# Twelve of sixteen gate projections of a merge, computed earlier and kept in DRAM

## The chip, the core and the metric

The kernel runs on one core of one Trainium2 chip. A core has a tensor engine (PE, with its weight load PEld), a vector engine (DVE), a scalar engine (ACT), GpSimd (POOL), and SyncE (SP), which issues most DMA transfers. Each engine works through its own instructions in a fixed order; semaphores tie them together. The metric is the device time of one execution in microseconds (us), lower is better. The kernel before takes 2801.38 us (median of 3 runs, 2801.16 to 2807.91).

## What is computed

512 tokens and 16 meta tokens of 1024 features go through two blocks; only the first block's mixer matters here. In float32, with RMS norms left out of the sketch:

```
z = norm(h) @ w_in
c_q, c_kv, k_pe, r_q, r_k, r_v, r_g, za, zr = split(z)
y_a = attention(c_q, c_kv, k_pe) @ w_mla_out      # 8 heads, causal, latent queries and keys
y_r = retention(r_q, r_k, r_v, r_g) @ w_ret_out   # 8 heads, in chunks of 128 tokens
merged = sigmoid(za) * y_a + sigmoid(zr) * y_r    # za, zr: [tokens, 1024]
h = h + merged @ w_mix_out
```

Then come an expert layer (128 x 128 experts, sixteen picked per head), a second block with three kinds of attention, and a feed-forward layer.

## The kernel before

Every activation lies as [128 features, tokens], 1024 features being 8 tiles. Every large product is done in three passes with operands split into a rounded high part and a low rest (`fm`, line 249: high x high, high x low, low x high), so a product of 128 columns of weights with 512 tokens is 3 x 8 = 24 matmuls. `wfm` brings a chunk of weights: SP loads it (line 222), ACT writes the high part (line 210), DVE or POOL in turn the low part (line 211). There are two buffers each of raw, high and low parts, and two PSUM banks `mm` for such products; a bank is free again when an engine has read the product.

The mixer, in the order of the program:

- The latent queries and keys (to about 62 us of the span).
- `ret_k(0)` to `ret_k(3)`: keys of two retention heads each. Two products of 24 matmuls (264 tokens each), a copy by ACT (line 621), four transfers between partitions issued by ACT (line 630), two products with rotation tables on DVE (lines 631, 632), POOL's sum into `rkf` (line 637), and four transposes on PE (line 640).
- Between them `mla_q(c)`: queries of four attention heads, four token tiles of nine matmuls (line 258), rotated by DVE and POOL (line 405), transposed (line 564); and `mla_kv(c)`: keys and values, five token tiles, whose norm needs a square root on ACT (line 594), products on DVE and POOL (line 598), transposes (line 603).
- `mla_attend(i, c)`: four token tiles i for each half c of the heads. Scores on PE (line 682), masked maxima on DVE (line 683), exponentials on ACT (line 694), scaling on DVE (line 700), small copies on POOL (line 701), transposes (lines 704, 713), copies (706, 715), and products with the values (708, 718). `ret_q(0)` to `ret_q(3)`, the retention's queries, stand before and among them.
- The retention's values and gate, then four chunks `ret_chunk(t)` of two half tiles each: scores `s` (line 769), DVE's mask (772), products `py` (778, 779), statistics (783, 784), normed `ry` on ACT and DVE (792, 795), transposes (799), a product on DVE (801), and the state's update (807, 810).
- The merge: for each of 8 column tiles c a gate of `za`, the attention's projection (12 matmuls), a gate of `zr`, the retention's projection (24 matmuls), and `merged`. A gate is 24 matmuls of the normed tokens `hn` and a tanh on ACT (line 831), since sigmoid is (1 + tanh of the half) / 2.

The functions write the instructions in this order; a scheduler then places each engine's instructions by its own estimate of when they are ready, so pieces of later steps come in between, and the order on an engine is fixed when the kernel runs. Names such as `mm`, `tp`, `s` and `o` are PSUM banks, `t` and `m` are tiles from the pools `t2` (5 buffers) and `mtwo` (9 buffers), which many short lives share: the scores of an attention tile take four of the nine.

Of the kernel before, what the change touches and what calls it, by code (L numbers as in the profile page):

```python
# [9 lines left out]
F32 = mybir.dt.float32  # L10
# [8 lines left out]
T = 512          # tokens whose outputs are wanted  # L19
M = 16           # meta tokens; in the key order they come after the tokens  # L20
# [6 lines left out]
GT = 3           # token tile whose experts are gathered; the others go through all experts  # L27
TD = 3 * P       # tokens that go through all experts
TB = 16          # tokens of one block of gates in DRAM
NTB = TD // TB  # L30
NE = 8           # e1's of one load of gates
SLOT = 8 * L     # words of a large slot


# ---------------------------------------------------------------- layout on the host
# [16 lines left out]
def _constants():  # L52
# [5 lines left out]
    tri01 = (q[None, :] >= q[:, None]).astype(f)                       # [m, c]  # L58
# [28 lines left out]
    c, s = (x.T.astype(np.float64) for x in _rope_tab(pos, 32))        # [32, token]  # L87
    lg = np.log(1.0 - 2.0 ** (-5.0 - np.arange(8)))
    e = lg[:, None] * pos[None, :]                                     # log of the decay since the start
    ret = np.zeros((8, P, 2, L))  # L90
    for x in range(8):                                                 # keys' pairs of heads, then queries'
        for b in range(2):
            d = np.exp(e[2 * (x % 4) + b])[None]
            d = d if x >= 4 else 64 ** -0.5 / d
            ret[x, b * 64:b * 64 + 64, 0] = np.concatenate([c, c], 0) * d
            ret[x, b * 64:b * 64 + 64, 1] = np.concatenate([-s, s], 0) * d
# [9 lines left out]
def _layout(i):  # L106
    i = {k: np.asarray(v) for k, v in i.items()}
    a = _constants()
    h = np.concatenate([i["x"][0], i["meta_tokens"]], 0)               # [528, 1024]
# [36 lines left out]
    pe = np.stack([i["pe_k_2"][0], i["pe_v_2"][0]], 0)                  # [2, 32, 64]  # L146
    pe = pe.transpose(2, 0, 1).reshape(64, 64)
    a["pe"] = np.ascontiguousarray(np.concatenate([pe, pe], 0))          # [(g dh), (k/v, l)]
    a["w_c1"] = np.stack([i[n][0].reshape(2, 16, 64, 256).transpose(0, 2, 1, 3).reshape(P, 16 * 256)  # half, dh, l, hidden
# [16 lines left out]
# ---------------------------------------------------------------- the program  # L166
def build(tc, A, OUT):
# [29 lines left out]
    # constants  # L197
# [10 lines left out]
    def split(src, hi, lo, lo_eng=None):  # L208
        """hi is src rounded to float32r, lo the rest."""
        S.copy(hi, src)  # L210
        (lo_eng or V).tensor_tensor(lo, src, hi.bitcast(F32), op=OP.subtract)  # L211
# [6 lines left out]
    def weights(ap, n, lo_pool=3, tag="w"):  # L218
        """One chunk of weights from DRAM, split in two float32r parts."""
# [14 lines left out]
    def wfm(name, c, kt=KD, width=P, c0=0):  # L234
        """some columns of weights, by tiles of features"""
        n = kt * width
        return kview(weights(A[name][c][:, c0:c0 + n], n, 2), kt, width)
# [7 lines left out]
    def fm(out, w, act, c0, t0, n, kt=KD, hooks=()):  # L245
        """out [128 columns of w, n tokens]; hooks: what comes after the first, the second pass"""
# [7 lines left out]
    def tm(out, w, act, c0, n, t0, m, kt=KD):  # L254
        """out [m tokens, n columns of w]"""
# [8 lines left out]
    def rstd_cols(sqs, n, width, out, first=0, after=None):  # L264
        """out[token, tile] = 1 / sqrt(mean over the features + eps) of the tokens from first up to n; sqs(t0, m):
        the squares of m tokens, [feature, token]; after: a factor of the tokens that comes first, and into out."""
# [17 lines left out]
    def ks(t):  # L284
        """the tiles [128, tokens] of t [128, k, tokens]"""
# [4 lines left out]
    class Squares:  # L290
        """sum of the squares of the tiles [128 features, n tokens] of the residual stream, as they come"""
# [3 lines left out]
        def add(self, x, eng=None, a=0, b=None, last=False):  # L295
            """the last tile's squares stay by themselves"""
# [12 lines left out]
    class Norm:  # L309
        """RMS norm over the features (partitions and tiles) of the tiles src, some tokens after the others;  # L310
        put(k, tile, a, b): tokens a .. b of a normed tile."""
        def __init__(self, src, sqs, g0, put, pieces=HALVES, dst=None):
# [3 lines left out]
            S.activation(self.col[:, 7:8], eps, AF.Sqrt)    # (its table is in place when the norm needs it)  # L316
            self.rowt = two(sqs.tp, "row")

        def cols(self, i):
            """1 / sqrt(mean + eps) of each token"""  # L320
# [3 lines left out]
        def row(self, i):  # L324
            """the same, along the partitions"""
# [31 lines left out]
    def by_halves(act, jobs, hooks=()):  # L357
        """products of act with columns of weights, jobs: (weights, first column, done(ps, a, b)); all jobs for
        half of the tokens, then for the other; hooks: what comes within the first product"""
# [7 lines left out]
    def residual(get, act, sqs=None, norm=None):  # L367
        """adds act's product with the weights get(k) (and their first column) to the residual stream; the last
        tiles by halves of the tokens, with the first half's norm among the products of the second"""
# [20 lines left out]
    def rope_op(dst, src, c, sn, sp, shape, tp, add=None):  # L390
        """dst = rotation of src, both [m, heads, 2 * half]; c, sn, sp: cos, -sin, sin"""
# [15 lines left out]
    def rope_tab(rope, off, w, m, h):  # L407
        """views of a packed table [cos | cos | -sin | sin], the same for each head"""
# [9 lines left out]
    def two(tp, name="t2", dt=F32):  # L418
        """a tile of 2 KB a partition, of a kind shared by many short lives"""
        return tp.tile([P, L], dt, name=name, tag="t2")  # L420

    # halves of arrays [feature, token]: the residual stream, and the experts' inputs
# [6 lines left out]
    hd = dp.tile([KD, P, T], F32, name="hd")                # the residual stream, while the experts run  # L429
    weight_pool(es, D)  # L430


    # ================================================================ first block: mixer
# [24 lines left out]
    # the latents come from the tokens before their norm, which goes into the latents' own: y = h gain / rms(h), and  # L458
    # rms of a latent c of y is sqrt(r^2 mean(c'^2) + eps), r = 1 / rms(h), c' = the latent of h gain
# [20 lines left out]
    # latent queries and keys, [feature, token], gained but not yet normed  # L480
# [27 lines left out]
    # shared rotary key, [token, 32]  # L508
# [25 lines left out]
    # four heads at a time: queries [96, head, token], their norm in the scale of the scores; keys  # L534
    # [96, head, (meta, token)]; values [token, head, 64]
# [4 lines left out]
    # the values of the meta tokens, one block of rows and columns per head  # L540
# [66 lines left out]
    # ---- retention: the decay since the start of the sequence is in the rotations' tables  # L607
    xh, qz = halves("rq", "xa")                             # queries of a head, zeros for the pair's other head
# [3 lines left out]
    kf = half_slot("rkf")                                   # keys [two heads' 64, pair, token]  # L612
    ktm = half_slot("rkt")[:, :, :T]                        # keys [token, tile (the last: meta), head's 64]

    def fm_pieces(w, pieces):
        """128 columns of w, [column, token]"""
# [7 lines left out]
    def ret_rope(x, j, n):  # L624
        """rotation of two heads [2 x 64, n tokens], the terms of a sum"""
# [23 lines left out]

    ret_k(0)  # L650
    mla_q(0)
    ret_k(1)
    va = flat(half_slot("va"), NT * 512).rearrange("p (t h d) -> p t h d", t=NT, h=8)
    mla_kv(0, va)
    ret_k(2)
    mla_q(1)
    ret_k(3)
    mla_kv(1, va)
    ret_q(0)
    pms = []  # L660
    for j in range(2):                                      # meta tokens' probabilities of four heads, zero elsewhere
# [6 lines left out]
    def mla_attend(i, c):  # L668
        """a tile of queries, four heads"""
# [946 lines left out]
```

## Time and profile before

| | |
|---|---|
| median of 3 runs | 2801.38 us |
| span of the profiled execution | 2800.6 us |
| PE busy | 2628.7 us, 94% |
| DVE busy | 1794.0 us, 64% |
| ACT busy | 1131.5 us, 40% |
| POOL busy | 1196.4 us, 43% |
| mixer, latent projections and first attention | about 60 to 230 us |
| retention's chunks | about 326 to 373 us |
| merge and output projection | about 373 to 560 us |

The page lists no time of the profiled execution beside its span; the median is 0.8 us above the span. A busy PE is a PE with a matmul under way: matmuls overlap, so the time from one start to the next says more than the length of one. The granted clock is that of PE as a share of 2.4 GHz; 0.5 is its lower level, 1.2 GHz. A wait in brackets is idle time of the engine ahead of the row and the instruction that ended it.

### The profile page before, as it was taken

What the parts mean: (1) busy time and instruction counts of PE and PEld (TensorE: products, weight loads), DVE (VectorE), ACT (ScalarE), POOL (GpSimd) and SP (SyncE); (2) the same over time, 40 slices, a digit from 0 to 9 for tenths busy, and PEclk for the clock granted to TensorE, in tenths of its full rate; (3) what the DMA queues carried; (4) which work ended last, traced back from release to release, by engine and by line L of the source; (5) the groups of instructions that cost most, each with busy time, mean ns of one, the idle gap of its engine ahead of it and who ended that gap; (6) DMA issues with size and microseconds to landing.
All of it is one profiled execution on the core that took longest, in us unless ns stands there. A gap on an engine that the chain in (4) does not pass through costs nothing.

```text
span 2800.6 us, 37220 instructions
## 1 busy us (share of the span) xinstructions
PE 2628.7 (94%) x13809; PEld 2246.1 (80%) x13809; DVE 1794.0 (64%) x3334; ACT 1131.5 (40%) x2064; POOL 1196.4 (43%) x831
## 2 busy tenths in 40 slices
PE   7889999998889799999999999998999999999998
PEld 6668778898789788888888888887666687878886
DVE  5673442259899736888988988896698521533333
ACT  4462343243777533333333333333566422422322
POOL 2322132325455926666666666662333333211111
PEclk9999999999999899999999999998999999999998
DMA  3312123322345467888888888884210132222221
GB/s 112 101 54 83 65 72 127 114 85 96 121 142 170 128 228 281 305 313 321 316 310 305 314 319 300 299 285 147 81 37 20 38 98 98 105 84 104 92 93 58
DMA packets 166149, 449.67 MB, mean 161 GB/s; under 512 B 14544, under 2 KB 67152, under 8 KB 159312
## 3 DMA queue, kind: packets, MB, share of 16 engines
q1 hardware_dynamic: 125648, 308.31, 32.0%
q0 software_dynamic: 36864, 134.23, 14.1%
q10 hardware_dynamic: 3456, 4.76, 0.7%
q8 instruction: 108, 1.77, 0.2%
q14 instruction: 73, 0.60, 0.1%
HBM read 413.10 MB, written 29.36 MB: 158 GB/s over the span
## 4 chain that ended last, share of the span: by engine, by line
PE 33%; DVE 22%; issue 9%; DMA 5%; POOL 4%; ACT 3%; ACTq 0%; DVEq 0%; SPq 0%; POOLq 0%
PE mm L249 21%; DVE vl L211 4%; PE py L1144 4%; PE pu L249 3%; DVE oh L1063 3%; DVE yg L958 2%; DVE row L948 2%; DMA row<-in_u_rows_dram,eg 2%; DMA row<-in_v_rows_dram,eg 2%; POOL oh L1038 1%; DVE al L211 1%; ACT ah L210 1%; PE tp L1469 1%; DVE act L1134 1%; PE o L1474 1%
## 5 line engine op out<-in xcount | busy, mean ns | idle before, releaser
L211 POOL TENSOR_TENSOR wl<-wr,wh 128x1024 fp32r<-128x1024 f32 (+1 forms) x199 | 480.7, 2416 | 572.6 <-ACT wh L210 277.2
L210 ACT CAST wh<-wr 128x1024 fp32r<-128x1024 f32 (+2 forms) x271 | 275.1, 1015 | 326.7 <-PE mm L249 213.3
L249 PE MATMUL pu<-xf,wh 128*128 128x384 f32 x2048 | 398.2, 345 | 0.4 <-ACT wh L210 0.4
L249 PEld LDWEIGHTS pu<-xf,wh 128*128 128x128 f32 x2048 | 366.2, 192 | 7.5 <-ACT wh L210 0.6
L210 ACT CAST ah<-act 128x384 fp32r<-128x384 f32 x128 | 65.9, 515 | 484.9 <-DVE act L1134 484.9
L211 DVE TENSOR_TENSOR al<-act,ah 128x384 fp32r<-128x384 f32 x128 | 201.7, 1576 | 79.6 <-ACT ah L210 78.3
L943 POOL DMA_INDIRECT row<-in_v_rows_dram,eg x128 | 193.6, 1512 | 132.6 <-DVE yg L958 101.5
L943 POOL DMA_INDIRECT row<-in_u_rows_dram,eg x128 | 185.4, 1449 | 130.8 <-DVE row L948 108.2
L1144 PE MATMUL py<-vh,ah 128*128 128x512 f32 x768 | 201.7, 397 | 26.7 <-ACT ah L210 26.6
L249 PE MATMUL pu<-xf,wl 128*128 128x384 f32 x1024 | 207.1, 344 | 5.3 <-POOL wl L211 5.3
L211 DVE TENSOR_TENSOR vl<-vr,vh 128x1024 fp32r<-128x1024 f32 x128 | 172.7, 1349 | 52.4 <-ACT vh L210 52.4
L1144 PE MATMUL py<-vl,ah 128*128 128x512 f32 x768 | 198.8, 394 | 0.0
L1144 PE MATMUL py<-vh,al 128*128 128x512 f32 x768 | 196.5, 390 | 0.0
L1144 PEld LDWEIGHTS py<-vh,ah 128*128 128x128 f32 x768 | 142.2, 189 | 60.3 <-ACT ah L210 37.7
L249 PEld LDWEIGHTS pu<-xf,wl 128*128 128x128 f32 x1024 | 184.4, 192 | 6.3 <-POOL wl L211 6.3
L958 DVE SCALAR_TENSOR_TENSOR yg<-row,ag,yg 128x1024 f32<-128x1024 f32 x127 | 167.9, 1322 | 16.4 <-DMA row<-in_v_rows_dram,eg 14.3
L948 DVE SCALAR_TENSOR_TENSOR row<-row,xg 128x1024 f32<-128x1024 f32 x128 | 168.4, 1346 | 10.8 <-DMA row<-in_u_rows_dram,eg 10.6
L1144 PEld LDWEIGHTS py<-vl,ah 128*128 128x128 f32 x768 | 146.2, 190 | 31.2
L1144 PEld LDWEIGHTS py<-vh,al 128*128 128x128 f32 x768 | 145.2, 189 | 30.4
L210 ACT CAST vh<-vr 128x1024 fp32r<-128x1024 f32 x128 | 134.3, 1049 | 78.8 <-DMA vr<-in_v_rows_dram 42.3
L1063 DVE TENSOR_TENSOR oh<-iota,eT 128x1024 f32<-128x1024 f32 x96 | 150.5, 1589 | 18.0 <-PE mm L1072 17.6
L211 POOL TENSOR_TENSOR wwl<-wwr,wwh 128x2048 fp32r<-128x2048 f32 x10 | 45.9, 4594 | 266.4 <-ACT wwh L210 266.4
(461 smaller groups left out, 5253.8 us busy)
## 6 DMA issues: line engine op xcount, KB each, us to landing
wr<-in_u_T_dram SPq DMA_DIRECT2D x128, 512.0 KB
vr<-in_v_rows_dram SPq DMA_DIRECT2D x128, 512.0 KB
wwr<-in_w_f_dram SPq DMA_DIRECT2D x32, 1024.0 KB
gates<-stg SPq DMA_DIRECT2D x24, 1024.0 KB
gin<-gates SPq DMA_DIRECT2D x16, 1536.0 KB
wr<-in_w_gm_dram SPq DMA_DIRECT2D x16, 512.0 KB
wr<-in_w_rv_dram SPq DMA_DIRECT2D x8, 512.0 KB
wr<-in_w_rg_dram SPq DMA_DIRECT2D x8, 512.0 KB
```

The source lines that it names most:

```text
L210: S.copy(hi, src)
L211: (lo_eng or V).tensor_tensor(lo, src, hi.bitcast(F32), op=OP.subtract)
L249: TE.matmul(out, w[a][k][:, c0:c0 + P], act[b][k][:, t0:t0 + n], start=i == 0 and k == 0, stop=i == 2 and k == kt - 1)
L943: G.indirect_dma_start(out=r, out_offset=None, in_=src, in_offset=bass.IndirectOffsetOnAxis(ap=eg[:, k:k + 1], axis=0))
L948: V.scalar_tensor_tensor(r, r, 1.0, xg, op0=OP.mult, op1=OP.mult, accum_out=ag[:, k:k + 1])
L958: V.scalar_tensor_tensor(yg[0], r, ag[:, k:k + 1], yg[0], op0=OP.mult, op1=OP.add)
L1038: G.tensor_tensor(ov[:, h], ov[:, h], iv[:, 4 * c + h, None].to_broadcast([P, 16, 16]), op=OP.mult)
L1063: V.tensor_tensor(a1, iota[:, None, None, :].to_broadcast([P, 2, 4, P]), eT[:, :2, b0 + q0:b0 + q0 + 4, None].to_broadcast([P, 2, 4, P]), ...
L1134: V.tensor_tensor(av, av, gated_acts.g[:, :, (e % NE) * TB:(e % NE + 1) * TB], op=OP.mult)
L1144: TE.matmul(py[2 * t + d], x[:, t * P:(t + 1) * P], w[:, d * 512:(d + 1) * 512], start=e == 0 and i == 0, stop=e == P - 1 and i == 2)
L1469: TE.transpose(pt[:, x * P:(x + 1) * P], sts[a][br][:, j * P:(j + 1) * P], ident)
L1474: TE.matmul(po[b * 64:b * 64 + 64, :2 * P], vt[:, j, br, g], pT[:, b * 256:b * 256 + 256], start=False, stop=last, skip_group_check=True)
```

## The change

`gate` is defined before the latent projections' loop. A generator `ahead` computes twelve gates, the eight of `za` and the first four of `zr`, into tiles of the pool `mtwo` and writes each (256 KB) to the DRAM tile `gz`. `fill(n)` takes the next n of them: one or two after most of the latent projections (six in all), one after every attention tile but the first of each half (six). In the merge `gate_of` reads a stored gate back from DRAM in place of computing it; the last four gates of `zr` are computed there as before. The rest of the difference takes comments and docstrings out and moves line numbers: line 640 of before is line 641 after, 564 is 565, 603 is 604, 621 is 622, 682 is 709, 778 is 808, 799 is 829; the tanh's line 831 is now 656.

```
+    gz = dp.tile([2, KD, P, T], F32, name="gz")
...
+    def gate(name, c, x):
+        w = wfm(name, c)
+        ps = mmps()
+        fm(ps, w, hn, 0, 0, T)
+        S.activation(x, ps, AF.Tanh, scale=0.5)
+        return x
+    AWAY = [(0, c) for c in range(KD)] + [(1, c) for c in range(4)]
+    def ahead():
+        for b, c in AWAY:
+            nc.sync.dma_start(gz[b, c], gate(("w_za", "w_zr")[b], c, mtwo("gz")[:, :T]))
+            yield
+    side = ahead()
+    def fill(n):
+        for _ in range(n):
+            next(side, None)
     ret_k(0)
     mla_q(0)
+    fill(1)
     ret_k(1)
     va = flat(half_slot("va"), NT * 512).rearrange("p (t h d) -> p t h d", t=NT, h=8)
     mla_kv(0, va)
+    fill(1)
     ret_k(2)
+    fill(1)
     mla_q(1)
+    fill(1)
     ret_k(3)
     mla_kv(1, va)
+    fill(2)
     ret_q(0)
...
     for c in range(2):
         for i in range(NT):
             mla_attend(i, c)
+            if i:
+                fill(1)
         ret_q(1 + c)
     ret_q(3)
+    fill(len(AWAY))
...
-    def gate(name, c, x):
-        w = wfm(name, c)
-        ps = mmps()
-        fm(ps, w, hn, 0, 0, T)
-        S.activation(x, ps, AF.Tanh, scale=0.5)
-        return x
...
+    def gate_of(b, c):
+        x = two(t2)[:, :T]
+        if (b, c) not in AWAY:
+            return gate(("w_za", "w_zr")[b], c, x)
+        nc.sync.dma_start(x, gz[b, c])
+        return x
     for c in range(KD):
-        x = gate("w_za", c, two(t2)[:, :T])
+        x = gate_of(0, c)
         gated("w_mla", c, oT, 4, x)
-        y = gate("w_zr", c, two(t2)[:, :T])
+        y = gate_of(1, c)
         gated("w_ret", c, yr, KD, y)
         merged(x, y, mg, c)
```

The first place is PE around the third retention key. In the kernel before, `mm_1067` is the second half of that key's product, `q_...` are the second round's queries (36 matmuls, of which the last nine are shown), `mm_1105` takes the key's transposes, and `mm_1253` is the fourth key:

```order
L249 MATMUL mm_1067<-hnh_159,wl_1037 128x264 x5
...
L258 MATMUL q_1212<-wh_1114,cqh_171 128x384 x2
L258 MATMUL q_1212<-wh_1120,cqh_171 128x384
L258 MATMUL q_1212<-wh_1114,cql_172 128x384 x2
L258 MATMUL q_1212<-wh_1120,cql_172 128x384
L258 MATMUL q_1212<-wl_1115,cqh_171 128x384 x2
L258 MATMUL q_1212<-wl_1121,cqh_171 128x384
L640 MATMUL mm_1105<-cstt_60,rkf_594 128x128 x3
L640 MATMUL mm_1105<-cstt_60,rkf_594 16x128
L564 MATMUL tp_1148<-cstt_60,m2_1138 96x128 x4
```

And now, where `mm_1136` is that half of the key's product, `mm_1174` takes its transposes, and `mm_1188` is a gate:

```order
L249 MATMUL mm_1136<-hnh_160,wl_1106 128x264 x8
L258 MATMUL q_1228<-wh_1217,cqh_172 128x384 x2
L258 MATMUL q_1257<-wh_1217,cqh_172 128x384 x2
L258 MATMUL q_1286<-wh_1217,cqh_172 128x384 x2
L641 MATMUL mm_1174<-cstt_60,rkf_595 128x128 x3
L641 MATMUL mm_1174<-cstt_60,rkf_595 16x128
L249 MATMUL mm_1188<-hnh_160,wh_1184 128x512 x8
L249 MATMUL mm_1188<-hnl_161,wh_1184 128x512 x4
L249 MATMUL mm_1188<-hnl_162,wh_1184 128x512 x4
L249 MATMUL mm_1188<-hnh_160,wl_1185 128x512 x8
L258 MATMUL q_1228<-wh_1223,cqh_172 128x384
```

Between the key's product and its transposes stand six matmuls of queries in place of thirty-six; the other thirty come behind a gate.

The second place is ACT just ahead of that, in the changed kernel alone. `mm_1076` is the second gate, `mm_1110` and `mm_1136` are the two halves of the third key's product, `rk` is the square root of the keys' norm, `kT` the copies of their transposes:

```order
L606 COPY kT_928<-tp_1031 96x4x128
L622 COPY t2_1109<-mm_1110 128x264
L595 ACTIVATE rk_1054<-rk_1054,epst_63 16x4
L656 ACT_TABLE_LOAD
L656 ACTIVATE gz_1069<-mm_1076 128x512
L606 COPY kT_928<-tp_1063 96x4x16
L210 CAST wh_1217<-wr_1215 128x768
L622 COPY t2_1109<-mm_1136 128x264
```

The tanh that frees the bank of `mm_1076`, which `mm_1136` takes over, stands behind the copy of `mm_1110`, a square root and the load of a table.

The third place is PE in the retention's chunks. `py` are the chunk's products, `s` the scores, `tp` the transposes; before, `mm_3550` is the attention's first projection and `mm_3571` the first gate of `zr`:

```order
L249 MATMUL mm_3550<-oTl_1522,wh_3546 128x512 x2
L249 MATMUL mm_3550<-oTh_1521,wl_3547 128x512 x4
L249 MATMUL mm_3571<-hnh_159,wh_3567 128x512 x4
L778 MATMUL py_3470<-rv_2260,sT_3468 128x128
L779 MATMUL py_3470<-wst_3421,rq_585 128x128
...
L799 MATMUL tp_3456<-cstt_60,ry_3451 128x128
L249 MATMUL mm_3571<-hnh_159,wh_3567 128x512 x2
L799 MATMUL tp_3456<-cstt_60,ry_3451 128x128
L249 MATMUL mm_3571<-hnh_159,wh_3567 128x512
```

And now, from the last matmul of that projection (`mm_3928`) on:

```order
L249 MATMUL mm_3928<-oTh_1726,wl_3925 128x512
L829 MATMUL tp_3675<-cstt_60,ry_3670 128x128 x2
L808 MATMUL py_3742<-rv_2669,sT_3740 128x128
L809 MATMUL py_3742<-wst_3735,rq_585 128x128
...
L799 MATMUL s_3779<-rq_586,rkf_595 128x256 x2
L829 MATMUL tp_3717<-cstt_60,ry_3712 128x128 x4
L808 MATMUL py_3784<-rv_2669,sT_3782 128x128
L809 MATMUL py_3784<-wst_3735,rq_586 128x128
```

The gates that lay between the chunk's steps are gone; from the fifth of the eight half tiles on, no matmul of another step stands between them.

## Rows read from the trace of the kernel before

**Rows 1.** Windows: length, busy (count) by engine, granted clock, DMA share, GB/s.

```profile
60.00:230.00 170.00, 150.41 (x960) 119.51 (x958) 110.40 (x335) 83.77 (x192) 48.95 (x68) 0.97 0.27 82
...
156.00:228.00 72.00, 67.26 (x457) 49.61 (x456) 51.84 (x182) 40.39 (x98) 17.49 (x37) 0.98 0.18 56
...
325.60:373.50 47.90, 46.04 (x304) 37.56 (x304) 35.31 (x118) 23.03 (x41) 12.51 (x9) 1.00 0.09 28
...
373.50:556.00 182.50, 179.82 (x792) 145.59 (x791) 42.50 (x50) 53.03 (x67) 53.46 (x32) 1.00 0.34 114
```

**Rows 2.** Waits of PE from 60 to 230 us: total, times, longest.

```profile
PE mm L640 <- POOL rkf L637: 6.2, 4, 2.5
PE tp L564 <- POOL m L405: 3.5, 2, 2.1
PE s L682 <- DVE mx L683: 3.3, 1, 3.3
PE tp L603 <- POOL m L598: 2.8, 4, 1.6
PE tp L603 <- DVE rk L593: 1.1, 1, 1.1
```

**Rows 3.** Timeline of PE: ends of key products, and their transposes.

```profile
88.71 1.16 PE L249 MATMUL mm<-hnh,wl 128*128 128x264 f32 x8
...
96.91 0.66 PE L640 MATMUL mm<-cstt,rkf 128*128 128x128 f32 x4 [1.47 <-POOL rkf L637]
...
107.84 0.86 PE L249 MATMUL mm<-hnh,wl 128*128 128x264 f32 x5
...
117.65 0.66 PE L640 MATMUL mm<-cstt,rkf 128*128 128x128 f32 x4 [0.67 <-POOL rkf L637]
```

**Rows 4.** Timeline of ACT: a copy, a square root, the table load, the next operation.

```profile
127.95 0.37 ACT L621 COPY t<-mm 128x264 f32<-128x264 f32 x1
...
152.57 0.30 ACT L594 ACTIVATE rk<-rk,epst 16x4 f32<-16x4 f32 x1 [0.73 <-DVE rk L593]
...
155.90 0.21 ACT L605 COPY kT<-tp 96x64 f32<-96x64 f32 x1
156.12 1.28 ACT L694 ACT_TABLE_LOAD   x1
157.42 0.51 ACT L694 ACTIVATE s<-s,mx,scq 128x144 f32<-128x144 f32 x1
```

**Rows 5.** Groups of ACT, 325 to 374 us: the gates' tanh.

```profile
L831 ACT ACTIVATE t<-mm 128x512 f32<-128x512 f32 x2 | 1.2, 599 | 0.0
```

**Rows 6.** Windows: granted clock (0.83) after a wait of 2.06 us.

```profile
80.00:90.00 10.00, 7.94 (x53) 7.80 (x53) 6.38 (x22) 3.21 (x7) 1.83 (x4) 0.83 0.42 146
```

**Rows 7.** Timeline of POOL: the low part of a weight chunk.

```profile
140.87 2.40 POOL L211 TENSOR_TENSOR wl<-wr,wh 128x1024 fp32r<-128x1024 f32 x1 [0.52 <-ACT wh L210]
```

**Rows 8.** Groups of DVE, then of ACT, 156 to 228 us: busy, mean ns.

```profile
L683 DVE CUSTOM_DVE_ANT_0 s<-s,cstt 128x512 f32<-128x512 f32 x8 | 5.5, 687 | 0.8 <-PE s L682 0.8
...
L700 DVE TENSOR_SCALAR s<-s,sm 128x528 f32<-128x528 f32 x8 | 3.5, 495 | 0.0
...
L694 ACT ACTIVATE s<-s,mx,scq 128x528 f32<-128x528 f32 x8 | 6.6, 828 | 0.4 <-DVE mx L690 0.3
```

**Rows 9.** Groups of DVE and PE in the retention, 325 to 374 us.

```profile
L783 DVE BATCH_NORM_STATS2 st<-py 128x6 f32<-128x128 f32 x32 | 8.0, 278 | 4.5 <-PE py L779 4.5
...
L772 DVE TENSOR_TENSOR sT<-s,cstt 128x512 f32<-128x512 f32 x8 | 5.3, 668 | 4.5 <-PE s L769 4.5
...
L249 PE MATMUL mm<-hnh,wl 128*128 128x512 f32 x17 | 5.4, 424 | 0.0
...
L249 PE MATMUL mm<-hnh,wh 128*128 128x512 f32 x16 | 5.0, 429 | 0.0
L249 PE MATMUL mm<-hnl,wh 128*128 128x512 f32 x16 | 4.9, 417 | 0.0
```

## The prediction, made before the changed kernel had run

> **What bounds the kernel now.** I read the page first, for its busy shares and its slices of the span: the tensor engine (PE) is busy for 94% of the span, so work that merely changes its place on PE gains nothing, and only PE's idle stretches and its clock are to be had. Then I cut the mixer into stages with the windows. From 373.5 to 556 us, where the gates and the branches' projections run today, 792 matmuls take 182.5 us and PE idles for 2.7 us [rows 1]: PE's own work sets the end there, at 182.5 / 792 = 0.23 us for a matmul of 512 columns (the last ones have 256, so this is slightly low). From 60 to 230 us, where the change puts twelve gates, PE idles for 170 - 150.4 = 19.6 us, at a mean granted clock of 0.97 [rows 1]. The waits of PE in that stretch name the causes: 6.2 us in four waits for the rotated retention key (written by POOL), 3.5 us for the rotated queries, 2.8 and 1.1 us for the normed keys of the attention, 3.3 us for the first softmax's maxima [rows 2]. The window at 80 us shows what such a wait does to the clock: 0.83, that is a third of ten microseconds at 1.2 GHz in place of 2.4 after a wait of 2 us, which loses about 1.7 us of matmuls [rows 6]; three windows of ten microseconds look like it, and 3% of 170 us is 5 us in all. So at most 19.6 + 5 = 24.6 us, 0.9% of the time, can be gained.
>
> **The change, part by part.** One gate is 24 matmuls, 24 x 0.23 = 5.5 us of PE; twelve are 66 us. They leave a place where PE is full and so take the whole 66 us off it (two of them lie in the retention's gaps, which is put right below); they enter the stretch before it, which grows by 66 us less what they fill. The sum is therefore over waits: those that go, those that stay, those that come. It is made against the profiled execution, whose span is 2800.6 us; the median of the runs shown, 2801.38, is 0.8 us more, which I keep as the part around the span.
>
> *Nothing by themselves:* twelve writes of 256 KB and twelve reads back. The DMA engines are at 0.27 and 0.34 of their time in the two stages [rows 1]; the reads stand ahead of their use by two steps of the merge, each 36 matmuls or 8.3 us. A write waits on SP for its tanh, and behind it stand weight loads and rotation tables; the tables have a further 5.7 us (48 matmuls of 264 columns, 0.23 x 264 / 512 each) before they are used, so I count 0. If that cover were gone, a weight load would be late by its own landing. The weight splits move with their gates; ACT and DVE have room (83.8 and 110.4 of 170 us [rows 1]). The merge stays full: of a step's 8.3 us POOL needs 2.4 for a low part [rows 7] and little beside.
>
> *Waits that go:* a gate stands among the transposes of the attention's keys in both rounds, where PE waited 2.8 + 1.1 us [rows 2]: -3.9.
>
> *Waits that stay:* the first rotated key, the first round of queries, and the second and fourth key behind the same four key-value tiles as before: 0. The second round of queries keeps a POOL low part of 2.4 us [rows 7] ahead of a rotation: 0.
>
> *A wait that grows, at the third key.* From the end of a key's product to its transposes it took 96.91 - 89.87 = 7.0 us (second key) and 117.65 - 108.70 = 8.95 us (third) [rows 3]: a copy, four transfers between partitions, two products, POOL's sum. Before, thirty-six query matmuls lay in between, and 0.67 us of wait remained. Now six do, about 1 us (384 columns each), since the gate's weights occupy the second of two buffers that the queries' need; the gate itself is queued behind the transposes. (7.0 + 8.95) / 2 - 1.0 - 0.67 = +6.3 (5.3 to 7.3). The low clock behind it, +1.7, I set against the stretch that should go with the softmax's wait, -1.7.
>
> *A wait that comes, before the second half of that key's product.* Its PSUM bank is the one that the second gate filled (there are two), and the gate's tanh stands on ACT behind the first half's copy, a square root and a table load: 0.37 + 0.30 + 1.28 [rows 4] + 0.60 [rows 5] = 2.55 us, with only this product queued behind it on PE: +2.6. Before, ACT loads one table between 60 and 170 us; now seven. In the row the load takes 1.28 us and the next operation starts 0.02 us later, and none of the time before it is idle [rows 4]. The Trainium skill ("ScalarE: Activation LUTs", What ACT_TABLE_LOAD costs) puts a drain of 1.38 us beside the 1.28 us for each switch of sets; by it this wait would be 3.9 us and the sum 1.3 us higher. The row shows no such drain, so the sum goes by the row.
>
> *The small transposes that end the second round of keys:* POOL now has a gate's low part, 2.4 us [rows 7], ahead of the product that they wait for. Between 0 and +2.4; neither end is nearer, so +1.2.
>
> *The attention.* Today the scores of two or three tiles run ahead of the first tile's transposes, and PE idles 72.0 - 67.3 = 4.7 us in 156 to 228 us [rows 1]. Now a gate stands between, and the next tile's scores come after this tile's transposes. For a last tile the gate gives 23 x 0.23 = 5.3 us of cover; the chain is four maxima of 0.69, an exponential of 0.83 and four scalings of 0.44 (3.5 / 8) [rows 8], 5.3 us without its small steps and hand-overs, which I estimate at 1 to 3 us. Two such tiles, 4 us, and some 2.5 us at the start, less 4.7: +2. Its ends: -4.7 if all is covered, +6 if every tile shows its hand-overs (four tiles with a gate more at 1 to 2 us).
>
> *The retention, whose fillers go.* From 325.6 to 373.5 us it has no slack on PE (1.9 us idle [rows 1]) only because the first two gates of the merge lie in its gaps: 48 of the 49 gate-shaped matmuls of the window [rows 9], 48 x 0.23 = 11.0 us. Those two gates are among the twelve. Behind them remain twelve matmuls of the first projection. What the stage gives back is at most what DVE waits there for PE, 4.5 + 4.5 us [rows 9]; it is busy for 35.3 of 47.9 us [rows 1], and each half tile is a chain over PE, DVE and ACT. So +2.0 to +11.0. I take +6, about the middle, since neither a full DVE nor an idle one is near.
>
> Sum: -3.9 + 6.3 + 2.6 + 1.2 + 2 + 6 = +14.2 us; 2801.4 + 14.2 = 2815.6.
>
> **Rivals.** *The gates cover the waits (faster).* While PE works at a gate, POOL, DVE and ACT come ahead, and each later wait shrinks. For it: 16.9 of the 19.6 us are waits [rows 2] for other engines that are at most two thirds busy. Against it: the gates stand behind several of these waits, not ahead. Place: the third key and the attention. Price: of the 19.6 us, 7.6 stay (6.2 for the keys less the third's 0.67, and 2.1 for a query [rows 2, 3]); 12 go, with 1.7 of clock: 2801.4 - 13.7 = 2788. It decides if the third key's wait stays under 2 us and the retention shrinks by the 9 us that DVE waits there. The Trainium skill ("TensorE: Matmul & The Clock Gate", What's actually happening) says that PE's activity releases its clock, which speaks for this rival; its worth here is the 5 us of clock above and is in that price only in part.
>
> *Nothing moves.* The waits filled and those that come are alike, within the 3.9 us of the keys and the 2.6 us of the table; the retention gives its 9 us back, and the third key's wait is half of mine: about 2801 + 5. For it: the same PE work in both kernels. Against it: three of the new waits can be read off the order.
>
> *Worse.* The retention gives nothing back, +11.0 in place of 6, and the attention +6 in place of 2, with one low-clock stretch of 1.7 us more after each: 2815.6 + 5 + 4 + 3.4 = 2828.
>
> *It doesn't do what it says:* the gates are issued early, but if the tiles' waits stand ahead of them on PE they fill nothing; that is in the first two items of my sum.
>
> **How the numbers follow.** A difference of 0.3%, 8.4 us, is what a measurement of this kernel can tell from no change. Forecast 0.47, by its own ends 2806 to 2827; worse 0.10; nothing moves 0.24; faster 0.19. Slower by over 0.3%: 0.44 of the forecast and the 0.10 of the worse case, 0.54; the remaining 0.03 of the forecast and nothing moves, 0.27; faster 0.19. The range that leaves a tenth on either side: 2794 to 2829.
>
> **What would show it.** In the changed kernel's waits of PE: one for the rotated key of 5 us or more, behind six query matmuls; one of 2 to 3 us for ACT's tanh of the second gate; seven table loads on ACT before the attention's end in place of one. In the windows: a retention stage with PE under 85% busy and some 5 us shorter; a merge shorter by 55 us and still full; the stage from 60 us longer by about 75 (66 and the new waits). Wrong would be: no key's wait over 3 us, or a retention that ends 9 us sooner. If the attention's windows show PE over 95% busy with DVE over two thirds, the loss of run-ahead was not one.

## The result and the profile after

The changed kernel takes 2836.39 us (median of 4 runs, 2832.75 to 2840.24) against 2804.64 us before (4 runs): a ratio of 1.0113, 95% interval 1.0096 to 1.0131. It is slower by 31.8 us, where 14.2 were forecast. The profiled execution has a span of 2838.1 us, 37.5 more than that of before. 34.5 of these lie between 60 us and the first product of the experts, where the change is; the other 3 come behind it, where both kernels run the same instructions, and where the traces of the kernels below differ by as much (2173.7 to 2180.6 us, with 2176.8 before and 2179.8 after).

This stretch, cut at the same events in both kernels (first attention scores, first retention scores, first product with the retention's output, first and last product of the output projection, first product of the experts), as windows of before:

```profile
60.00:147.80 87.80, 74.55 (x456) 62.99 (x454) 51.95 (x134) 39.36 (x87) 28.37 (x28) 0.96 0.33 105
147.80:325.70 177.90, 169.72 (x1074) 137.72 (x1073) 84.34 (x241) 75.59 (x156) 38.88 (x47) 0.99 0.22 70
325.70:372.70 47.00, 45.14 (x300) 36.84 (x299) 34.68 (x117) 22.23 (x41) 12.51 (x9) 1.00 0.09 29
372.70:515.90 143.20, 142.67 (x615) 114.98 (x614) 33.47 (x37) 42.65 (x53) 35.93 (x22) 1.00 0.34 111
515.90:564.30 48.40, 46.25 (x253) 39.58 (x253) 12.36 (x18) 15.62 (x21) 17.53 (x10) 1.00 0.36 123
564.30:623.80 59.50, 56.14 (x422) 54.17 (x421) 29.01 (x100) 23.42 (x54) 16.71 (x11) 0.91 0.23 73
```

and of after (length; busy time and count of PE, PEld, DVE, ACT, POOL; granted clock; DMA share; GB/s):

```profile
60.00:192.30 132.30, 108.84 (x578) 89.20 (x577) 53.14 (x142) 57.39 (x108) 35.02 (x31) 0.91 0.30 93
192.30:415.50 223.20, 214.43 (x1238) 170.40 (x1237) 86.19 (x238) 85.58 (x166) 44.71 (x50) 0.98 0.27 86
415.50:459.40 43.90, 37.60 (x249) 28.31 (x247) 34.14 (x116) 15.50 (x33) 9.99 (x7) 0.99 0.11 33
459.40:549.20 89.80, 89.75 (x377) 72.06 (x378) 24.29 (x33) 26.38 (x34) 33.10 (x18) 0.97 0.42 135
549.20:599.10 49.90, 47.75 (x254) 40.74 (x253) 12.35 (x18) 15.63 (x21) 17.53 (x10) 0.97 0.35 120
599.10:658.30 59.20, 55.83 (x422) 53.87 (x421) 28.83 (x100) 23.34 (x54) 16.72 (x11) 0.91 0.22 74
```

The matmuls are the same (3120 and 3118 records), yet PE's busy time grows from 534.5 to 554.2 us, by 19.7; its idle time (length less busy) grows from 29.3 to 44.1, by 14.8. So more than half of the loss is matmuls that take longer. Most of that is the clock. In windows of about 5 us, busy time times (1 less the granted clock) sums to 8.8 us before and 21.1 after: +12.3 of the 19.7 (with the windows cut elsewhere, 8.4 to 9.4 and 20.7 to 22.0). The largest group of matmuls shows it, here over the whole stretch, first before, then after:

```profile
L249 PE MATMUL mm<-hnh,wh 128*128 128x512 f32 x224 | 61.2, 406 | 0.5 <-ACT t L831 0.5
```

```profile
L249 PE MATMUL mm<-hnh,wh 128*128 128x512 f32 x224 | 69.7, 448 | 0.2 <-ACT wh L210 0.2
```

The same 224 matmuls take 8.5 us more. They are the first pass of every product of 512 tokens; 128 of them begin a gate, and a gate now often begins behind a wait.

A second cut says where. From retention and merge in before and in e3 below, (47.0 + 143.2 - 47.1 - 76.2) / 12 = 5.58 us is what a gate costs PE. Ahead of the retention's scores the stretch grew by 89.8 us, less 12 x 5.58 = 66.9: 22.9 lost. From there to the experts it shrank by 55.3 (298.1 to 242.8): 11.6 of the 66.9 were not given back.

The waits of PE from 60 to 420 us after, to be held against [rows 2]:

```profile
PE mm L641 <- POOL rkf L638: 15.1, 4, 7.7
PE tp L604 <- POOL m L599: 4.7, 6, 2.6
PE tp L565 <- POOL m L405: 3.8, 3, 1.9
PE tp L731 <- POOL pm L728: 2.6, 4, 1.2
PE tp L770 <- ACT t L622: 2.1, 1, 2.1
PE tp L604 <- DVE rk L593: 1.2, 2, 0.6
```

The rotated key costs 15.1 us in place of 6.2. Its longest wait is the third key's, with all engines in order of time (ACTq and SPq: DMA issues):

```profile
126.12 1.32 PE L258 MATMUL q<-wh,cqh 128*128 128x384 f32 x6
126.22 0.38 ACT L622 COPY t<-mm 128x264 f32<-128x264 f32 x1
...
126.63 3.21 ACTq L631 DMA_DIRECT2D t<-t  x4
126.63 2.17 DVE L632 TENSOR_TENSOR t<-t,t 128x528 f32<-128x528 f32 x1 [3.46 <-ACT t L622]
...
133.02 0.71 DVE L633 TENSOR_TENSOR t<-t,t 128x528 f32<-128x528 f32 x1 [4.22 <-DMA t<-t]
133.81 1.29 POOL L638 TENSOR_TENSOR rkf<-t,t 128x528 f32<-128x528 f32 x1 [5.58 <-DVE t L633]
...
135.16 1.12 PE L641 MATMUL mm<-cstt,rkf 128*128 128x128 f32 x4 [7.72 <-POOL rkf L638]
...
135.93 3.76 PE L249 MATMUL mm<-hnh,wh 128*128 128x512 f32 x8
...
139.49 2.58 PE L249 MATMUL mm<-hnl,wh 128*128 128x512 f32 x8
...
141.91 2.02 PE L249 MATMUL mm<-hnh,wl 128*128 128x512 f32 x8
```

Read downwards, this is the chain of copy, transfers, product, sum; PE stands for 7.72 us, as forecast (the wait grew by 7.05 us against the 0.67 of [rows 3]; 6.3 were said). What was not in the sum stands in the last three rows: the gate behind the wait runs its first eight matmuls in 3.76 us and the next in 2.58, where a full clock takes 2.02. The granted clock from 135 to 140 us is 0.50, 1.2 GHz:

```profile
135.00:140.00 5.00, 4.84 (x14) 3.90 (x15) 0.74 (x2) 0.00 (x0) 0.10 (x1) 0.50 0.00 0
```

### The profile page after: what moved, and what is told of

Its sections match the earlier page's. It is cut to its first block, busy times and chain, and to the rows that moved or that the text cites. A ratio compares the mean times of both kernels' runs of the same rounds, so it can differ in the third digit from the quotient of the medians.

```text
span 2838.1 us, 37263 instructions
## 1 busy us (share of the span) xinstructions
PE 2650.2 (93%) x13809; PEld 2256.5 (80%) x13809; DVE 1793.3 (63%) x3334; ACT 1135.0 (40%) x2068; POOL 1202.4 (42%) x831
## 3 DMA queue, kind: packets, MB, share of 16 engines
q8 instruction: 108, 1.77, 0.3%
## 4 chain that ended last, share of the span: by engine, by line
PE 31%; DVE 21%; issue 10%; DMA 5%; POOL 5%; ACT 3%; ACTq 0%; DVEq 0%; SPq 0%; POOLq 0%
PE mm L249 21%; DVE vl L211 4%; DVE row L977 3%; PE pu L249 3%; DVE oh L1092 3%; DMA row<-in_u_rows_dram,eg 3%; PE py L1173 3%; DVE yg L987 2%; DMA row<-in_v_rows_dram,eg 2%; POOL oh L1067 1%; PE tp L1498 1%; ACT ah L210 1%; DVE act L1163 1%; PE o L1503 1%; DVE s L1486 1%
## 5 line engine op out<-in xcount | busy, mean ns | idle before, releaser
L210 ACT CAST wh<-wr 128x1024 fp32r<-128x1024 f32 (+3 forms) x271 | 274.5, 1013 | 329.5 <-PE mm L249 212.8
L977 DVE SCALAR_TENSOR_TENSOR row<-row,xg 128x1024 f32<-128x1024 f32 x128 | 173.2, 1384 | 12.5 <-DMA row<-in_u_rows_dram,eg 12.3
```

Of the source, the lines that this page charges most:

```text
L977: V.scalar_tensor_tensor(r, r, 1.0, xg, op0=OP.mult, op1=OP.mult, accum_out=ag[:, k:k + 1])
```

## The experiments

Theory A: the gates leave waits uncovered ahead of them and make some longer, and behind each longer wait the clock is low. Theory B: the loss is the retention without its two gates. Theory C: every gate's trip (DRAM, queue, table loads) costs a share. The results together, by the two cuts of the traces; "ahead" is the length from 60 us to the retention's first scores less that of before (265.7) less 5.58 per gate, "behind" the same from there to the experts' first product (before 298.1); idle and slow are PE's from 60 us to the experts, slow by windows of about 5 us as above:

| kernel | gates | median less before, us | ratio, 95% | ahead | behind | idle | slow |
|---|---|---|---|---|---|---|---|
| before | 0 | | | 0 | 0 | 29.3 | 8.8 |
| after | 12 | +31.8 | 1.0096-1.0131 | +22.9 | +11.6 | 44.1 | 21.1 |
| e1 | 6 | +16.6 | 1.0048-1.0082 | +19.2 | -0.4 | 40.8 | 13.9 |
| e2 | 6 | +6.5 | 1.0012-1.0035 | +8.4 | +1.8 | 33.6 | 11.9 |
| e3 | 12 | +17.1 | 1.0042-1.0082 | +18.7 | +0.2 | 41.3 | 11.2 |
| e4 | 12 | +20.7 | 1.0059-1.0103 | +10.3 | +11.6 | 38.0 | 14.7 |
| e5 | 12 | +16.1 | 1.0036-1.0070 | +6.3 | +12.1 | 35.2 | 14.3 |
| e6 | 6 | +3.0 | 1.0004-1.0023 | +4.8 | +1.6 | 33.4 | 11.7 |
| e8 | 12 | +22.3 | 1.0063-1.0096 | +21.6 | +7.9 | 42.7 | 20.3 |
| e9 | 0 | -4.4 | 0.9981-0.9999 | -3.6 | 0 | 29.5 | 7.8 |
| e11 | 6 | +6.1 | 1.0010-1.0029 | +6.4 | +1.7 | 31.1 | 11.0 |

The last four columns come from one trace each and carry its noise. The kernels before, e2 and e11 run the same 713 matmuls in the same order from 0 us to the attention's first scores, and reach these at 147.8, 149.0 and 149.8 us: differences of 2 us say nothing. The traced execution of before (span 2800.6 us) was a fast one: in the other kernels the time is about 2 us more than the span, which would make it 2802.6 for a median of 2804.64. So "ahead" and "behind" add up to 1 to 4 us more than the medians differ, in e8 to 7 more. The change of e9 lies ahead of 60 us; its "ahead" is by how much all that follows comes sooner.

**e1, e2, e3: each place alone.**

```
-    AWAY = [(0, c) for c in range(KD)] + [(1, c) for c in range(4)]
+    AWAY = [(0, c) for c in range(1, 7)]       # e1: no fill in the attention; e2: none in the latents
+    AWAY = [(0, c) for c in range(1, KD)] + [(1, c) for c in range(1, 6)]       # e3
```

> Six gates only (columns 1 to 6 of za), all among the latent projections at the places of the changed kernel; none among the attention tiles, and the merge's first two gates (za 0, zr 0) stay where they filled the retention's gaps. Theory A (waits for the rotated key and the normed key grow there, and the matmuls behind each wait run slower at a lower clock): the stage up to the first attention scores shows the key's waits of the changed kernel (about 15 us in four) and the time is 18 to 22 us over the kernel before, about 2822 us. Theory B (the loss is the retention without its two gates): within 6 us of before, about 2805. Theory C (each gate's trip through DRAM, its queue and table loads cost a share): half of 32, about 2817.

> Six gates only (columns 1 to 6 of za), all among the attention tiles, one after each tile but the first of a half; none among the latent projections; za 0 and zr 0 stay in the merge. Theory A: no key's wait is touched, the attention had 4.7 us of idle time which a gate may fill: 0 to +4 us over before, about 2803. Theory B: about 2801. Theory C: half of 32, about 2817.

> Twelve gates at the changed kernel's places, but others: za 1 to 7 and zr 1 to 5, so that za 0 and zr 0 are computed in the merge again and can fill the retention's gaps. Theory A: the latents' loss stays, the retention's and what follows at a lower clock (about 12 us in the traces) goes: 2836 - 12, about 2824. Theory B: nearly all goes, about 2806. Theory C: nothing goes, about 2836.

e1 lost 16.6 us, a little under theory A's 18 to 22 and as much as the 16 that C's half of 32 would be: its time does not separate the two. PE waits 14.6 us for the rotated key there, as A says. e2 lost 6.5, with an interval of 3.4 to 9.8: about A's upper end or more, and far less than C's 16. e3 gave 14.7 us back of the changed kernel's loss, A's 12 and a little. Its windows of retention and merge:

```profile
411.30:458.40 47.10, 45.24 (x300) 36.93 (x299) 34.62 (x117) 21.85 (x41) 12.51 (x9) 1.00 0.12 44
458.40:534.60 76.20, 75.68 (x326) 60.91 (x325) 21.73 (x31) 22.43 (x29) 29.19 (x16) 1.00 0.48 157
```

With the two gates back, the retention is as long and as full as before, and nothing is lost behind it. So the loss has two shares, 17 to 19 us that twelve gates cost with the fillers kept, and about 10 for the fillers; B alone and C are out. The 10 are the 11.6 behind the retention's first scores less some 1.7 of slow clock in the output projection, which stands in the column "behind" of e2, e6 and e11 too, whose retention kept its gates. The rest of the 14.7 lies in the attention, 223.1 us in the changed kernel and 219.3 in e3: slow clock costs 4.2 us there in the one and nothing in the other, and why stays open. The two places do not add up: e1's six gates cost 16.6 us, e2's six 6.5, and e3's twelve 17.1.

**e4: a key's transposes behind the next gate** (abridged).

```
     def ret_k(j): ...                 # product, rotation, sum
+    def ret_kt(j): ...                # the transposes
...
     ret_k(0); mla_q(0); fill(1)
+    ret_kt(0)
     ret_k(1); mla_kv(0, va); fill(1)
+    ret_kt(1)
     ret_k(2); fill(1); mla_q(1)
+    ret_kt(2)
     fill(1); ret_k(3); mla_kv(1, va); fill(1)
+    ret_kt(3)
+    fill(1)
```

> The changed kernel with its twelve gates, but each key's four transposes are issued behind the next gate (of the third key behind the gate and the queries) in place of ahead of it, so that the gate's 24 matmuls cover the chain of copy, transfers, products and sum. Theory A: the waits for the rotated key fall from 15.1 us to under 4, the slow matmuls behind them go too (6 to 8 us): about 2836 - 18 = 2818. Theories B and C: the same gates, the same traffic, the same retention, so within 4 us of 2836.

The first two rows of PE's waits in e4, 60 to 420 us:

```profile
PE tp L604 <- POOL m L599: 10.1, 6, 4.2
PE tp L565 <- POOL m L405: 5.6, 4, 1.8
```

The rotated key's wait is gone from the list, and the kernel is 10.8 us faster than the changed one, with the same gates and the same traffic: the order was the cause of that much, as A says. But 18 were expected. Of the 15.1 us of waiting 7.2 come back at the normed key and the queries (4.7 + 3.8 before this edit, 10.1 + 5.6 now), the next in line, and 3.3 more at three waits that were not there (1.4, 1.2 and 0.7).

**e5, e6: POOL's queue.** In `gate`, the weights' low part always by DVE; e6 with AWAY as in e1 and no fill in the attention.

```
-        w = wfm(name, c)
+        w = kview(weights(A[name][c], KD * P, V), KD, P)
```

> The kernel of e4, with the low part of every gate's weights written by DVE in place of DVE and POOL in turn. In e4 the waits for the normed key grew to 10.1 us in six, for POOL's sum, and a gate's low part of 2.4 us stood ahead of it on POOL. Theory D (POOL's queue is what now ends last): these waits fall to about 5 us, 2820 us. Theory E (DVE and POOL slow each other, DVE's low part took 2.82 us beside POOL's and 1.23 alone, so the work only changes its place): within 2 us of e4, 2825.

> The kernel of e5 with only six gates (za 1 to 6), all among the latent projections, the retention's two gates left in the merge. Theory A: what e1 lost (16.6 us) less the key's waits (11 us between the changed kernel and e4) and less about 4 us for POOL's queue: about 2 us over before, 2807 against 2805. If a gate's place in the latents costs whatever the order, it stays at 2821 as e1.

e5's median is near the one that D said (2821.5), but not for D's reason: the normed key's waits are 9.6 us, as in e4. Against e4 its 4.0 us are not clear of the noise, as the two intervals overlap. Neither theory is shown there. In e6 these waits are 12.5 us in all, the most of any kernel here; the longest:

```profile
107.85 2.35 POOL L211 TENSOR_TENSOR wl<-wr,wh 128x1024 fp32r<-128x1024 f32 x1 [2.72 <-PE kv L258]
...
108.48 2.81 DVE L211 TENSOR_TENSOR wl<-wr,wh 128x1024 fp32r<-128x1024 f32 x1 [1.00 <-PE mm L249]
...
111.21 0.16 DVE L596 RECIPROCAL rk<-rk 128x4 f32<-128x4 f32 x1
...
113.00 1.05 PE L604 MATMUL tp<-cstt,m 128*96 128x128 f32 x4 [4.19 <-POOL m L599]
```

DVE's low part begins beside POOL's, takes 2.81 us where 1.23 is usual, and the key's reciprocal stands behind it. It ends 1.09 us after POOL's, as does the one that starts at 116.25 us in the changed kernel beside POOL and takes 1.77: it stood while POOL worked. (The Trainium skill, "SBUF — State Buffer", SBUF: two separate sides, says that these two engines share a port pair which one holds for a whole instruction while the other blocks; the rows agree.) e6 came out as forecast, 2808.5 for 2807: six gates in a good order, with their low parts on DVE, cost 3.0 us, in the order of e1 16.6.

**e7, e9: idle time and the clock.** Matmuls whose product nobody reads: in e7 in the changed kernel at the third key, in e9 in the kernel before, in the 6.05 us wait at 46 us (`busy` is the same loop, into the bank that the attention uses later; abridged). A call shows as two matmuls in the trace, so eight are x16.

```
+        if j == 2:                                            # e7, in ret_k
+            idle = bank("o", "idle")
+            for _ in range(8):
+                TE.matmul(idle, ident, x[:, :T], start=True, stop=True)
...
+                if wname == "w_ckv" and not k and a:          # e9, in latent
+                    busy(h1[0][:, :T], 6)
```

> The changed kernel with eight matmuls added whose product nobody reads, between the third key's product and its transposes, so that PE is busy while it would wait 7.7 us. If it is the idle time that takes the clock down: no low clock behind them, the gate's first eight matmuls in 1.9 us in place of 3.76, and the same start of the transposes. If the clock falls for another reason (a place in time, the form of the transposes): 3.76 us as before.

> The kernel before, with six matmuls added whose product nobody reads, where PE waits 6.05 us for ACT among the first latents (46 us). Nothing else is changed. If idle time takes the clock down, as in e7: the clock of 45 to 55 us goes from 0.51 and 0.81 to 1.00, and about 3.4 us of slow matmuls go (5 x 0.49 + 5 x 0.19): 2805 - 3.4 = 2801.6, the stretch to 60 us shorter by as much. If the low clock there had another cause, or the added matmuls delay what ACT and DVE are waiting for: the same time or up to 1 us more.

e7 (a single run, 2837.68 us; the trace is what counts), third key:

```profile
127.66 7.13 PE L642 MATMUL idle<-t,cstt 128*128 128x512 f32 x16
...
135.48 0.66 PE L646 MATMUL mm<-cstt,rkf 128*128 128x128 f32 x4 [0.69 <-POOL rkf L643]
...
135.89 2.11 PE L249 MATMUL mm<-hnh,wh 128*128 128x512 f32 x8
...
137.84 2.02 PE L249 MATMUL mm<-hnl,wh 128*128 128x512 f32 x8
...
139.69 2.02 PE L249 MATMUL mm<-hnh,wl 128*128 128x512 f32 x8
```

and the clock of the same window:

```profile
135.00:140.00 5.00, 4.52 (x22) 3.75 (x23) 0.74 (x2) 0.11 (x1) 0.42 (x1) 1.00 0.00 0
```

The transposes start when they did (135.48 for 135.16), no work was saved, and the gate behind them now runs its first eight matmuls in 2.11 us in place of 3.76, the next in 2.02 in place of 2.58: the slow matmuls were the price of PE's idle time, and it is a price beside the wait. (The Trainium skill, "TensorE: Matmul & The Clock Gate", What's actually happening, says that activity releases a throttled clock; this is that rule seen from the other side.) The experts begin 2.5 us sooner than in the changed kernel (655.77 for 658.32). In e9 the windows of before

```profile
45.00:50.00 5.00, 3.80 (x17) 3.80 (x18) 1.48 (x7) 1.08 (x3) 1.12 (x3) 0.51 0.00 0
50.00:55.00 5.00, 5.00 (x37) 5.00 (x36) 0.49 (x1) 1.87 (x4) 0.00 (x0) 0.81 0.01 3
```

become

```profile
45.00:50.00 5.00, 4.09 (x30) 3.46 (x29) 1.81 (x7) 1.31 (x4) 3.59 (x7) 1.00 0.00 0
50.00:55.00 5.00, 5.00 (x45) 4.86 (x45) 2.12 (x3) 2.46 (x5) 0.00 (x0) 1.00 0.02 7
```

and the kernel takes 2800.68 us against 2805.05, ratio 0.9990 (0.9981 to 0.9999), for 3.4 forecast. It is the one version that beats both kernels, by 0.3 to 5.3 us, and it needs none of the change. The trace does not put it all down to this wait: up to the attention's first scores it is 5.2 us shorter, 2.6 of them slow clock behind waits of 2.06 and 2.52 us that e9 has too (2.08 and 2.57) and that took nothing there, and 1.6 are lost again in the attention.

**e8: other work in the retention's gaps.** The attention's projections of the merge, two columns ahead (abridged).

```
+    mla_out(0); mla_out(1)
     for c in range(KD):
-        x = gate_of(0, c)
-        gated("w_mla", c, oT, 4, x)
+        if c + 2 < KD:
+            mla_out(c + 2)            # gate_of(0, c) and gated("w_mla", ...)
+        x = xm[c]
```

> The changed kernel with the attention's projections of the merge issued two columns ahead, so that 36 matmuls of them stand among the retention's chunks in place of 12. Theory A (the retention lost work that filled its gaps, whatever work it was): the 24 more matmuls, 5.6 us, vanish in the gaps, and the low clock at the merge's start (2.8 us) with them: 2836 - 7 = 2829. If the gaps are set by DVE and ACT so that nothing fits or the retention grows by what is put in: 2836.

```profile
414.20:460.30 46.10, 41.22 (x274) 32.23 (x272) 35.08 (x119) 16.89 (x36) 11.60 (x8) 1.00 0.14 49
460.30:543.40 83.10, 83.10 (x352) 66.70 (x353) 22.53 (x29) 25.06 (x32) 30.87 (x17) 0.98 0.41 140
```

25 more matmuls in the retention's window make it 2.2 us longer and the merge 6.7 shorter. By median the kernel is some 9 us faster than the changed one, where 7 were said, but only 5 of them lie ahead of the experts' first product in the traces (653.3 for 658.3); the rest is not explained by the edit. Other work than the gates fits into the retention's gaps, though not all of it for nothing.

**e10, e11: two that settled little.** e10 loads each gate's weights twice (the edit doubled the second block's gates too, since they use the same function, so only its mixer counts); e11 is e2 with its last gate between `ret_q(2)` and `ret_q(3)`.

> The changed kernel with the weights of the twelve gates loaded twice in a row. The transfers of the second key landed 3.8 us after the last was issued, of the third 3.2, in the kernel before 1.9 for the second, while a gate's weights came in. If those transfers share the DMA engines with the gate's weights: with 512 KB more in flight they land 1 us or more later, and the waits for the rotated key grow from 15.1 to about 17 us or more. If they are late for a reason of the engines' queues: 15 us again.

> The kernel of e2 (six gates among the attention tiles) with the last gate between the last two queries of the retention in place of ahead of both. In e2 a wait of 2.9 us for ACT's copy of the first values stood behind them: ACT's transfers for the last query wait there for a buffer, the copy behind the transfers. Theory A: with a gate between them that wait falls under 0.5 us and the slow matmuls behind it (1.7 us) go: 2811 - 4 = 2807. If the attention's gates cost by themselves: 2811 again.

In e10 the key's waits grew to 19.5 us, but the transfers of the second key landed 3.15 us after their last issue, not later than the 3.8 of after, and the second load stood on SP until the first had landed, so there was never more in flight. It shows nothing on sharing; why the second key's chain takes 9.2 us (94.9 to 104.15) for the 7.0 of [rows 3] stays open. In e11 the wait for ACT's copy went, as A said, and a wait of 2.0 us for DVE's copy of a value, 1.7 in the kernel before, stands in its place: 2811.1, as e2. A's number was wrong.

## Why the prediction was wrong

The direction was right and the time 21 us short, outside the range. Step by step:

- **The step that failed** is the clock: "The low clock behind it, +1.7, I set against the stretch that should go with the softmax's wait, -1.7." So the clock counted for nothing in the sum, where each wait left standing or new could have a price. Measured, slow clock costs 12.3 us more than before, more than any wait. The softmax's stretch did go (1.7 before), but slow stretches follow the waits of the second key (clock 0.50 from 105 to 110 us, 2.8 us in all), the third (0.50, 2.8), the small transposes (0.53 from 195 us, 3.1), the first value (1.3) and the retention's end with its many short ones (0.50 from 460 us, 2.9); the fourth key's (0.67) had one before. e7 shows for the third key that PE's idle time is the cause; for the others it is argued from their place behind a wait. [rows 6] had the price; it was netted away. A further 7.4 us of longer matmuls are not in the granted clock of these windows. About 4 of them lie in the retention, where 51 matmuls fewer, 11.7 us at 0.23, took only 7.5 off PE's busy time. I did not settle them; gates cut into pieces among transposes would be a candidate for the others, argued, not shown.
- **The idle time** came out at +14.8 us for +14.2 in the sum, but partly by luck:
  - Third key: +7.05 for +6.3; right, and e4 shows that order made it.
  - Second key: the cover was unchanged as said, the chain was not: 3.42 us for 1.47 [rows 3], +1.95 for 0.
  - The normed key's waits "that go" went by 1.0 us, not 3.9; the small transposes behind POOL's low part cost +2.9 for 1.2 (a low part of 2.46 us at 192.63, the norm's product at 195.05, PE at 195.82 after 2.58 of wait).
  - The wait for the second gate's tanh did not exist. PE waited 0.83 us at 122.12 for ACT's copy of the key's first half, and the tanh came later:

```profile
121.69 0.38 ACT L622 COPY t<-mm 128x264 f32<-128x264 f32 x1
...
122.12 1.25 PE L249 MATMUL mm<-hnh,wh 128*128 128x264 f32 x8 [0.83 <-ACT t L622]
122.28 1.28 ACT L656 ACT_TABLE_LOAD   x1
...
123.57 0.60 ACT L656 ACTIVATE gz<-mm 128x512 f32<-128x512 f32 x1
```

  The product took the bank that the copy had freed, not the gate's: I had assumed the two banks to alternate. There are seven table loads on ACT from 60 to 192 us, as said; none shows as a wait of PE.
  - Attention: no run-ahead was missed, the softmax's 3.3 us went, and 2.1 came at the first value, which was not in the sum: ACT's transfers for the last query start when POOL's sum for the query before has freed a buffer, and the copy stands behind them:

```profile
312.82 1.79 POOL L649 TENSOR_TENSOR rq<-t,t 64x512 f32<-64x512 f32 x1 [0.63 <-DVE t L633]
...
314.65 2.44 ACTq L631 DMA_DIRECT2D t<-t  x4
317.21 0.38 ACT L622 COPY t<-mm 128x264 f32<-128x264 f32 x1 [6.92 <-DMA wr<-in_w_rv_dram]
...
317.64 0.44 PE L770 MATMUL tp<-cstt,t 128*128 128x128 f32 x2 [2.12 <-ACT t L622]
```

- **The retention**: it gave back 3.1 us of 11, so +7.9 for +6, inside its ends (4.4 of it idle time of PE, the rest among the longer matmuls above); with the slow start of the merge (0.97 over 90 us, 2.8 us) the loss is about 10, and e3 returns it. The 1.6 to 1.7 of slow clock in the output projection that make it 11.6 are not the retention's: the same wait of 2.15 to 2.25 us for ACT stands there in every trace, and the clock behind it fell to 0.66 to 0.70 in nine of thirteen, e2, e6 and e11 among them, and stayed at 1.00 in four, before and e3 among them. PE is busy for 85.6% of the stage; "under 85" was a near miss.
- **The rivals**: the "worse" one (2828, chance 0.10) named the right ingredients, low clock after each wait and a retention that gives nothing back, and was still too mild. The gates as cover (2788) fell at the point that I had named, a third key under 2 us; only with the transposes moved (e4, e6) do they cover anything, and then the next chain shows.

## What to carry to other kernels

Work moved into a stretch full of waits fills a wait only if it stands between the product and the instruction that waits, on the waiting engine; look that up in the order first, and then price what it took along from where it was filler. Put a price on a long wait of PE twice: the wait, and the slow matmuls that may follow it, here 1.3 to 3.1 us behind waits of 2.1 to 7.7 us. For waits of 2 to 3 us the second price is a chance: it was paid in some of these kernels and not in others. A few matmuls for nothing in a wait that can't be filled took the second price away in e7 and e9.

## What was not expected of the hardware

- The clock does not fall after every wait of the same size: behind the 2.1 us at the first value it fell to 0.82 and 0.84 in the changed kernel and stayed at 1.00 in e3, which has the same wait; behind waits of 2.06 and 2.52 us it fell to 0.77 and 0.73 in the kernel before and stayed at 1.00 in e9, whose waits are 2.08 and 2.57.
- The reverse: six matmuls for nothing over 5.3 us kept the clock up through a wait of 6.2 us, with 0.91 us of it left idle (e9).
